# A hybrid decoder layer on one core: column blocks of the output projection paired at its begin and its end, and the last product in 256-column matmuls

## The chip, the core and the metric

The kernel runs on one core of a Trainium2 chip. Its engines are TensorE (PE, with its weight loads shown apart as PEld), VectorE (DVE), ScalarE (ACT), GpSimd (POOL) and SyncE (SP), which issues most of the DMAs. The metric is the device time of one execution in microseconds. Before the change the median of three runs was 1169.38 us (1169.16 to 1171.19).

## The reference

One layer over 256 tokens of width 2048, float32. What matters is the chain of four large products and the two layer norms, here in short:

```python
u = x @ w_in                                     # 2048 -> 6160, the first product
conv_out = conformer_conv_group(u[..., :1024], u[..., 1024:2048], ...)
gdn_out = gated_deltanet_group(u[..., c0:c1], u[..., c1:c2], ...)   # 8 heads, chunks of 64 tokens
mix = concat([conv_out, gdn_out]) @ w_out        # 2048 -> 2048, the second product
x = layer_norm(alpha * x + mix, ln1_g, ln1_b)
gu = x @ w_gate_up                               # 2048 -> 11264, the third product
hid = silu(gu[..., :D_FF]) * gu[..., D_FF:]      # D_FF = 5632
ffn = hid @ w_down                               # 5632 -> 2048, the fourth product
x = layer_norm(alpha * x + ffn, ln2_g, ln2_b)
```

Depth is 1, alpha is 2 to the power 0.25.

## The kernel before

Every large product is made of three matmuls on split operands: each float32 operand is cut into a high part (rounded to the type that TensorE takes) and a low part (what is left), and high by high, high by low and low by high are summed in PSUM.

**Weights.** A weight chunk is 256 rows by 512 columns, 512 KB. `wchunk` (L85 to L104) loads it by a DMA from SP into `wraw` (three buffers), ACT makes the high part `whi` (L93), DVE the low part `wlo` (L100); `whi` and `wlo` have four buffers each. A `wraw` buffer is free again when DVE has made the low part, a `whi` buffer when PE has used it. A program-wide scheduler orders the instructions of each engine by priority; weights are placed some 500 places ahead of their use (WPRI). Small pieces of the token mixer are queued with due times and run between chunks (`at`, `tick`, `require`).

**Second product.** Tokens (two halves `tk` of 128) are the stationary operand, 512 weight columns move. Its sum over 2048 rows is done in two passes: pass 0 takes the DeltaNet half (`mixg`), pass 1 the convolution half (`mixc`). `gemm2` (L723) runs one column block `nb` with four chunks `c`, both token halves in two PSUM banks `g2a`, `g2b`. Chunks 2 and 3 of pass 0 need the heads 4 to 7: `require(("gc"[pas], c // 2))`, which runs `head_mix` with its transposes `poT` (L615).

The last two column blocks of pass 1 are done differently (L802 to L829): all eight chunks stay in SBUF, those of block 2 in the four `whi`/`wlo` buffers, those of block 3 in four buffers of their own, `wxhi`/`wxlo`. Then token half 0 is run through blocks 2 and 3 (PSUM tiles `g2t`), its layer norm is started (`x1_stats`, `x1_norm`), and token half 1 is run through the same chunks, while the normed half 0 is transposed (`x1_turn`, tile `px1T`) to be the moving operand of the third product. The first chunks of the third product (`fxraw`, `fxhi`, `fxlo`, then `whi`) are loaded after those of the second.

**Third product.** Weights are stationary, 256 tokens move: 128x256 matmuls (L901), 22 column groups.

**Fourth product.** Tokens stationary again, 512 weight columns move (`tok_mm`), four column blocks of 22 chunks each, banks `g4a` and `g4b`, `evac4` adds the residual and takes the statistics. In the last block six chunks are held in SBUF: token half 0 is finished first and normed and stored (`finish`) while half 1 is multiplied, then half 1 is finished.

Of the kernel before, what the change touches and what calls it, by code (L numbers as in the profile page):

```python
# [14 lines left out]
P = 128  # L15
# [45 lines left out]
def hybrid_layer(ctx: ExitStack, tc, xT, xn, w1, wba, w2, w3, w4, pvec, consts, hrow, lrow, out):  # L61
# [18 lines left out]
    def mmt(name="mmt"):  # L80
        return mm.tile([P, 512], F32, tag="mm", name=name)
# [21 lines left out]
    def wchunk(src, split=False, into=None):  # L103
        return wrest(wload(src, split, into))  # L104
# [80 lines left out]
    def tick():  # L185
        while todo and todo[0][0] <= clock[0]:
            run_next()
        clock[0] += 1
# [3 lines left out]
    def require(key):  # L192
        while key not in done:
            run_next()
# [521 lines left out]

    def act_g(kt):
        return mixb[0][:, 0, kt, :], mixb[0][:, 1, kt, :]
# [4 lines left out]
    def gemm2(pas, nb):  # L723
        banks = [mmt("g2a"), mmt("g2b")]
        for c in range(4):
            hi, lo = wchunk(w2[pas, nb, c])
            require(("gc"[pas], c // 2))
            for k2 in range(2):
                for tk in range(2):
                    tok_mm(banks[tk], act_c if pas else act_g, 2 * c + k2, tk, hi, lo, k2, 8)  # L730
            tick()
        return banks
# [10 lines left out]
    for nb in range(4):  # L743
        banks = gemm2(0, nb)
        for tk in range(2):
            ysl = y[:, tk, nb * 512:nb * 512 + 512]
            STT(ysl, ysl, ALPHA, banks[tk], op0=ALU.mult, op1=ALU.add)
# [16 lines left out]
    for nb in range(2):  # L764
        banks = gemm2(1, nb)
        for tk in range(2):
            evac2(nb, tk, banks[tk])
# [3 lines left out]
    def x1_stats(tk):  # L771
        with tc.high_priority(offset=LPRI):
            m, r, nmr = ln_scalars(st1[:, tk], f"a{tk}")
            STT(nmr, m, -1.0, r, op0=ALU.mult, op1=ALU.mult)
        return m, r, nmr
# [26 lines left out]
    ws = {}  # L802
    for nb in (2, 3):
        for c in range(4):
            into = [pc.tile([P, 2, 512], F32R, tag=t, name=t, bufs=4) for t in ("wxhi", "wxlo")] if nb == 3 else None
            ws[nb, c] = wchunk(w2[1, nb, c], into=into)
    first = []
    for tk in range(2):
        for nb in (2, 3):
            if tk and nb == 3:  # L810
                for c in range(NF):
                    into = None
                    if c < NX:
                        into = [pc.tile([P, 2, 512], dt, tag=t, name=t, bufs=NX)
                                for t, dt in (("fxhi", F32R), ("fxlo", F32R), ("fxraw", F32))]
                    with tc.issue_after(loads[0].ins):
                        first.append(wload(w3[0, c], into=into))
            bank = mmt("g2t")
            for kt in range(8):
                tok_mm(bank, act_c, kt, tk, *ws[nb, kt // 2], kt % 2, 8)  # L820
                if tk and (nb, kt) in X1T:
                    with tc.issue_after(last[0].ins):
                        x1_turn(0, 4 * X1T.index((nb, kt)), 4)
            evac2(nb, tk, bank)
        sc1 = x1_stats(tk)
        hold = x1_norm(tk, 0, *sc1)
        if tk == 0:
            for b in range(1, 4):
                x1_norm(tk, b, *sc1)  # L829
# [89 lines left out]
    st2 = cp.tile([P, 2, 4, 6], F32, name="st2")  # L919
# [7 lines left out]
    def evac4(nb, tk, bank):  # L927
        sl = y[:, tk, nb * 512:nb * 512 + 512]
        STT(sl, sl, ALPHA, bank, op0=ALU.mult, op1=ALU.add)
        nc.vector.bn_stats(st2[:, tk, nb, :], sl)  # L930

    def finish(tk):
        m, r, _ = ln_scalars(st2[:, tk], f"b{tk}")
        for nb in range(4):
            sl = y[:, tk, nb * 512:nb * 512 + 512]
            STT(sl, sl, m, l2[:, 0, nb, :], op0=ALU.subtract, op1=ALU.mult)
            STT(sl, sl, r, l2[:, 1, nb, :], op0=ALU.mult, op1=ALU.add)
            nc.sync.dma_start(out[tk * P:tk * P + P, nb * 512:nb * 512 + 512], sl)

    NC4 = FT // 2  # L940
    wx = big.tile([P, 2, 2, 2, 512], F32R, tag="big", name="wx")
    for nb in range(4):
        banks = [mmt("g4a"), mmt("g4b")]
        held = 6 if nb == 3 else 0
        for c in range(NC4 - held):
            hi, lo = wchunk(w4[nb, c])
            for k2 in range(2):
                for tk in range(2):
                    tok_mm(banks[tk], act_h, 2 * c + k2, tk, hi, lo, k2, FT)
        ws = []  # L950
        for c in range(NC4 - held, NC4):
            i = c - (NC4 - held)
            ws.append(wchunk(w4[nb, c], into=(wx[:, i, 0], wx[:, i, 1]) if i < 2 else None))
        for tk in range(2):
            for kt in range(FT - 2 * held, FT):
                tok_mm(banks[tk], act_h, kt, tk, *ws[kt // 2 - NC4 + held], kt % 2, FT)
            evac4(nb, tk, banks[tk])
            if held:
                finish(tk)
# [10 lines left out]
NH0 = 1  # L970
X1T = [(2, 7), (3, 2), (3, 4), (3, 7)]
# [79 lines left out]
```

## Time and profile before

| | |
|---|---|
| median of 3 runs | 1169.38 us |
| profiled execution | 1173.28 us, its span 1171.5 us |
| PE busy | 1153.6 us (98%), 8514 matmuls |
| DVE, ACT, POOL busy | 63%, 48%, 3% |
| first product | 5.3 to 332 us |
| second product | 334 to 436 us |
| third product | 437 to 918 us |
| fourth product | 918 to 1160 us, then norm and store to 1171.5 us |

The profiled execution was 3.9 us slower than the median of the runs. PE is busy nearly all the time; a matmul's duration in the trace reaches past the start of the next one (they are pipelined), so a pace is read from start to start and not from a duration. Idle time in brackets names what ended it.

### The profile page before, as it was taken

The numbers are of one execution on the slowest core, as the hardware profiler recorded it, in microseconds if no ns is written. First come the engines' busy times: TensorE is split into PE (matmuls) and PEld (weight loads), VectorE is DVE, ScalarE is ACT, GpSimd is POOL, SyncE is SP. The second block draws the span as 40 slices with busy tenths as digits, with TensorE's granted clock in tenths as the row PEclk, the third lists the DMA queues.
The fourth block names the chain that finished last, engine by engine and source line by source line (L and its number), as shares of the span: only waits on it lengthen the run. The fifth ranks groups of instructions, "written<-read, shape, count | busy, mean of one in ns | idle before, by whom it ended". The sixth has DMA issues, their size and how long they took to land.

```text
span 1171.5 us, 20710 instructions
## 1 busy us (share of the span) xinstructions
PE 1153.6 (98%) x8514; PEld 1087.4 (93%) x8514; DVE 735.6 (63%) x1092; ACT 561.3 (48%) x803; POOL 34.9 (3%) x44
## 2 busy tenths in 40 slices
PE   9999999999999999999999999999999999999996
PEld 9999999999988879999999999999999888888884
DVE  5998998978847777545545455455554445454545
ACT  6567455556664544444444444444444333333340
POOL 1001011100000000000000000000000000000000
PEclk9999999999999999999999999999999999999998
DMA  8556564453535744655555555555555755555552
GB/s 292 182 190 214 176 210 156 153 196 127 198 129 177 263 150 159 217 191 192 197 195 191 194 195 197 191 191 196 197 194 192 264 187 190 197 189 189 197 202 86
DMA packets 62014, 222.65 MB, mean 190 GB/s; under 512 B 7168, under 2 KB 7680, under 8 KB 61280
## 3 DMA queue, kind: packets, MB, share of 16 engines
q1 hardware_dynamic: 58464, 208.37, 52.4%
q0 software_dynamic: 2160, 10.88, 2.8%
q10 hardware_dynamic: 1296, 2.10, 0.5%
q8 instruction: 66, 1.08, 0.4%
q14 instruction: 28, 0.23, 0.1%
HBM read 216.86 MB, written 4.46 MB: 189 GB/s over the span
## 4 chain that ended last, share of the span: by engine, by line
PE 71%; ACT 1%; DVE 1%; issue 1%; DMA 1%; POOL 0%; DVEq 0%; ACTq 0%
PE g3b L901 20%; PE g3a L901 20%; PE g4b L715 3%; PE g4a L715 3%; PE g4a L714 3%; PE g4b L714 3%; PE g4b L713 3%; PE g4a L713 3%; PE g1a L206 1%; PE g1b L206 1%; PE g2a L715 1%; PE g2a L713 1%; PE g2b L713 1%; PE g2a L714 1%; PE g2b L715 1%; PE g2b L714 1%
## 5 line engine op out<-in xcount | busy, mean ns | idle before, releaser
L100 DVE TENSOR_TENSOR wlo<-wraw,whi 128x1024 fp32r<-128x1024 f32 (+1 forms) x386 | 469.8, 1218 | 392.3 <-ACT whi L93 390.3
L93 ACT ACTIVATE whi<-wraw 128x1024 fp32r<-128x1024 f32 (+1 forms) x386 | 406.9, 1056 | 498.5 <-PE g3b L901 232.1
L901 PE MATMUL g3b<-x,whi 128*128 128x256 f32 x1344 | 261.7, 276 | 0.0
L901 PE MATMUL g3a<-x,whi 128*128 128x256 f32 x1344 | 261.6, 276 | 0.0
L901 PEld LDWEIGHTS g3a<-x,whi 128*128 128x128 f32 x1344 | 202.3, 188 | 0.0
L901 PEld LDWEIGHTS g3b<-x,whi 128*128 128x128 f32 x1344 | 202.3, 188 | 0.0
L901 PE MATMUL g3a<-x,wlo 128*128 128x256 f32 x672 | 130.8, 276 | 0.0
L901 PE MATMUL g3b<-x,wlo 128*128 128x256 f32 x672 | 130.8, 276 | 0.0
L639 DVE SCALAR_TENSOR_TENSOR cacc<-hh,pv,cacc 128x255 f32<-128x255 f32 (+27 forms) x240 | 100.8, 463 | 0.7 <-ACT cacc L636 0.7
L901 PEld LDWEIGHTS g3a<-x,wlo 128*128 128x128 f32 x672 | 101.2, 188 | 0.0
L901 PEld LDWEIGHTS g3b<-x,wlo 128*128 128x128 f32 x672 | 101.1, 188 | 0.0
L206 PE MATMUL g1a<-x_hi,whi 128*128 128x256 f32 x384 | 79.8, 290 | 0.9 <-ACT whi L93 0.5
L206 PE MATMUL g1b<-x_hi,whi 128*128 128x256 f32 x384 | 76.6, 281 | 0.0
L206 PE MATMUL g1a<-x_lo,whi 128*128 128x256 f32 x384 | 76.5, 281 | 0.0
L206 PE MATMUL g1b<-x_lo,whi 128*128 128x256 f32 x384 | 76.5, 281 | 0.0
L206 PE MATMUL g1a<-x_hi,wlo 128*128 128x256 f32 x384 | 76.4, 281 | 0.0
L206 PE MATMUL g1b<-x_hi,wlo 128*128 128x256 f32 x384 | 76.3, 280 | 0.0
L715 PE MATMUL g4b<-whi,hid 128*128 128x512 f32 x172 | 67.8, 394 | 0.0
L715 PE MATMUL g4a<-whi,hid 128*128 128x512 f32 x172 | 67.8, 394 | 0.0
L714 PE MATMUL g4a<-wlo,hid 128*128 128x512 f32 x172 | 67.4, 392 | 0.0
L714 PE MATMUL g4b<-wlo,hid 128*128 128x512 f32 x172 | 67.4, 392 | 0.0
L713 PE MATMUL g4a<-whi,hid 128*128 128x512 f32 x172 | 66.8, 388 | 0.0
(319 smaller groups left out, 1519.2 us busy)
## 6 DMA issues: line engine op xcount, KB each, us to landing
wraw<-in_w SPq DMA_DIRECT2D x388, 512.0 KB, 3.3
y<-in_xn POOLq DMA_DIRECT2D x1, 2048.0 KB, 8.5
rows<-in_lrow POOLq DMA_DIRECT2D x2, 1024.0 KB, 6.9
l<-in_lrow POOLq DMA_DIRECT2D x2, 1024.0 KB, 7.7
out<-y SPq DMA_DIRECT2D x8, 256.0 KB, 2.6
xr<-in_xT ACTq DMA_DIRECT2D x7, 256.0 KB, 5.4
wraw<-in_w SPq DMA_DIRECT2D x4, 256.0 KB, 4.1
dzx<-zbg POOLq DMA_DIRECT2D x2, 512.0 KB, 4.9
```

Of the source, the lines that this page charges most:

```text
L93: ACT(hi[:, k], raw[:, k], AF.Copy)
L100: TT(lo[:, k], raw[:, k], hi[:, k].bitcast(F32), op=ALU.subtract)
L206: last[0] = MM(o, lhsT=w[:, k2, ct * P:ct * P + P], rhs=r[:, kt, :], start=(kt == 0 and ct % 2 == 0 and r is r_hi and not fin), stop=(fin ...
L639: STT(a[:, s:], hh[:, i, :S - s], pcol(w + TAPS - 1 - s), a[:, s:], op0=ALU.mult, op1=ALU.add)
L713: MM(bank, lhsT=a_hi[:, tsl], rhs=hi[:, k2, :], start=(kt == 0), stop=False)
L714: MM(bank, lhsT=a_hi[:, tsl], rhs=lo[:, k2, :], start=False, stop=False)
L715: last[0] = MM(bank, lhsT=a_lo[:, tsl], rhs=hi[:, k2, :], start=False, stop=(kt == n - 1))
L901: last[0] = MM(banks[ct // 2][:, (ct % 2) * S:(ct % 2) * S + S], lhsT=w[:, k2, ct * P:ct * P + P], rhs=x1[kt // 8][:, kt % 8, part, :], st ...
```

## The change

Three edits. First, `gemm2` takes a tuple of column blocks and runs chunks 0 and 1 of all of them before chunks 2 and 3; the first two blocks of pass 0 are given as a pair. Second, at the end of pass 1 the eight chunks of blocks 2 and 3 are loaded and used, for token half 0, in an order of a table that mixes both blocks; token half 1 keeps its order. Third, the fourth product uses `half_mm`, in which each 512-column matmul is two of 256 columns, and in the held part of the last block token half 1 is finished in column halves; statistics of token half 1 are taken over 256 columns, and its last column block is normed and stored in two pieces.

```diff
+    def half_mm(banks, act, kts, tks, hfs, hi, lo, n):
+        for part, w in ((0, hi), (1, hi), (0, lo)):
+            for kt in kts:
+                for hf in hfs:
+                    cs = slice(hf * 256, hf * 256 + 256)
+                    for tk in tks:
+                        last[0] = MM(banks[tk][:, cs], lhsT=act(kt)[part][:, tk * P:tk * P + P], rhs=w[:, kt % 2, cs],
+                                     start=(kt == 0 and hf == 0 and part == 0 and w is hi),
+                                     stop=(w is lo and kt == n - 1), skip_group_check=True)
...
-    def gemm2(pas, nb):
-        banks = [mmt("g2a"), mmt("g2b")]
-        for c in range(4):
...
+    def gemm2(pas, nbs):
+        banks = {}
+        for half in range(2):
+            for nb in nbs:
+                if half == 0:
+                    banks[nb] = [mmt("g2a"), mmt("g2b")]
+                for c in (2 * half, 2 * half + 1):
+                    hi, lo = wchunk(w2[pas, nb, c])
+                    require(("gc"[pas], half))
...
-    for nb in range(4):
-        banks = gemm2(0, nb)
+    for nbs in ((0, 1), (2,), (3,)):
+        banks = gemm2(0, nbs)
...
+LASTW = [(2, 0), (3, 0), (2, 1), (2, 2), (3, 1), (2, 3), (3, 2), (3, 3)]
...
+    for nb, c in LASTW:
+        into = [pc.tile([P, 2, 512], F32R, tag=t, name=t, bufs=4) for t in ("wxhi", "wxlo")] if nb == 3 else None
+        ws[nb, c] = wchunk(w2[1, nb, c], into=into)
+    first = []
+    last_banks = {nb: mmt("g2t") for nb in (2, 3)}
+    for nb, c in LASTW:
+        for k2 in range(2):
+            tok_mm(last_banks[nb], act_c, 2 * c + k2, 0, *ws[nb, c], k2, 8)
+        if c == 3:
+            evac2(nb, 0, last_banks[nb])
...
-    st2 = cp.tile([P, 2, 4, 6], F32, name="st2")
+    st2 = [cp.tile([P, 4, 6], F32, name="st2a"), cp.tile([P, 8, 6], F32, name="st2b")]
...
-            for k2 in range(2):
-                for tk in range(2):
-                    tok_mm(banks[tk], act_h, 2 * c + k2, tk, hi, lo, k2, FT)
+            half_mm(banks, act_h, (2 * c, 2 * c + 1), (0, 1), (0, 1), hi, lo, FT)
...
+        for tk, hfs in ((0, (0, 1)), (1, (0,)), (1, (1,))):
+            for c in range(NC4 - held, NC4):
+                half_mm(banks, act_h, (2 * c, 2 * c + 1), (tk,), hfs, *ws[c - NC4 + held], FT)
+            evac4(nb, tk, banks[tk], hfs if tk else None)
+            if tk == 0:
+                finish(0, (0, 512, 1024, 1536, 2048))
+    finish(1, (0, 512, 1024, 1536, 1792, 2048))
```

The order of instructions shows where each part lands. First PE at the begin of the second product, pass 0, from the last matmul of block 0's chunk 1 to the first transpose `poT`. Before; `g2a_4380` and `g2b_4381` are block 0, `g2a_4514` and `g2b_4515` block 1:

```order
L715 MATMUL g2b_4381<-whi_4459,mixg_4088 128x512
L713 MATMUL g2a_4514<-whi_4517,mixg_4088 128x512
L714 MATMUL g2a_4514<-wlo_4518,mixg_4088 128x512
L715 MATMUL g2a_4514<-whi_4517,mixg_4088 128x512
L713 MATMUL g2b_4515<-whi_4517,mixg_4088 128x512
L714 MATMUL g2b_4515<-wlo_4518,mixg_4088 128x512
L715 MATMUL g2b_4515<-whi_4517,mixg_4088 128x512
L713 MATMUL g2a_4514<-whi_4517,mixg_4088 128x512
L615 MATMUL poT_4432<-con_81,vs_3702 128x128
```

And the same place with the change, where block 1 is `g2a_4476` and `g2b_4477`:

```order
L715 MATMUL g2b_4381<-whi_4459,mixg_4088 128x512
L713 MATMUL g2a_4476<-whi_4479,mixg_4088 128x512
L714 MATMUL g2a_4476<-wlo_4480,mixg_4088 128x512
L715 MATMUL g2a_4476<-whi_4479,mixg_4088 128x512
L713 MATMUL g2b_4477<-whi_4479,mixg_4088 128x512
L714 MATMUL g2b_4477<-wlo_4480,mixg_4088 128x512
L715 MATMUL g2b_4477<-whi_4479,mixg_4088 128x512
L713 MATMUL g2a_4476<-whi_4479,mixg_4088 128x512
L615 MATMUL poT_4432<-con_81,vs_3702 128x128
```

Nothing moved up to `poT`: the scheduler had put block 1's first chunk there before, too. What moves stands behind it.

Second, ACT at the end of the second product: the high parts of the eight chunks of blocks 2 and 3 (`whi` is block 2, `wxhi` block 3), between the last chunk of block 1 (`whi_4949`) and the first of the third product (`fxhi`). Before:

```order
L93 ACTIVATE whi_4949<-wraw_4948 128x1024
L93 ACTIVATE whi_4973<-wraw_4972 128x1024
L93 ACTIVATE whi_4979<-wraw_4978 128x1024
L93 ACTIVATE whi_4985<-wraw_4984 128x1024
L93 ACTIVATE whi_4991<-wraw_4990 128x1024
L93 ACTIVATE wxhi_4996<-wraw_4998 128x1024
L93 ACTIVATE wxhi_5002<-wraw_5004 128x1024
L93 ACTIVATE wxhi_5008<-wraw_5010 128x1024
L93 ACTIVATE wxhi_5014<-wraw_5016 128x1024
L93 ACTIVATE fxhi_5127<-fxraw_5129 128x1024
```

With the change:

```order
L93 ACTIVATE whi_4949<-wraw_4948 128x1024
L93 ACTIVATE whi_4973<-wraw_4972 128x1024
L93 ACTIVATE wxhi_4978<-wraw_4980 128x1024
L93 ACTIVATE whi_4985<-wraw_4984 128x1024
L93 ACTIVATE whi_4991<-wraw_4990 128x1024
L93 ACTIVATE wxhi_4996<-wraw_4998 128x1024
L93 ACTIVATE whi_5003<-wraw_5002 128x1024
L93 ACTIVATE wxhi_5008<-wraw_5010 128x1024
L93 ACTIVATE wxhi_5014<-wraw_5016 128x1024
L93 ACTIVATE fxhi_5127<-fxraw_5129 128x1024
```

The first load of block 3 stands second instead of fifth, and the last of block 2 sixth instead of fourth; SP's queue has the same order.

Third, DVE behind that, from the low part of the eighth chunk to the begin of the norm of token half 0 (L753, now L768, adds a PSUM bank to `y`). Before:

```order
L100 TENSOR_TENSOR wxlo_5015<-wraw_5016,wxhi_5014 128x1024
L100 TENSOR_TENSOR fxlo_5128<-fxraw_5129,fxhi_5127 128x1024
L753 TENSOR_TENSOR y_4378<-y_4378,g2t_5047 128x512
L100 TENSOR_TENSOR fxlo_5133<-fxraw_5134,fxhi_5132 128x1024
L754 BN_STATS st1_4806<-y_4378 128x6
L100 TENSOR_TENSOR wlo_5139<-wraw_5137,whi_5138 128x1024
L736 BN_AGGR mva0_5074<-st1_4806 128x2
```

With the change:

```order
L100 TENSOR_TENSOR wxlo_5015<-wraw_5016,wxhi_5014 128x1024
L100 TENSOR_TENSOR fxlo_5128<-fxraw_5129,fxhi_5127 128x1024
L768 TENSOR_TENSOR y_4378<-y_4378,g2t_5020 128x512
L100 TENSOR_TENSOR fxlo_5133<-fxraw_5134,fxhi_5132 128x1024
L769 BN_STATS st1_4806<-y_4378 128x6
L768 TENSOR_TENSOR y_4378<-y_4378,g2t_5021 128x512
L769 BN_STATS st1_4806<-y_4378 128x6
L750 BN_AGGR mva0_5074<-st1_4806 128x2
```

Block 2's addition and statistics, which stood further ahead, now stand behind the low part of the eighth chunk, and `wlo_5139` has gone behind the norm's first steps.

## Rows read from the trace of the kernel before

**Rows 1.** The page: busy time and share; DVE's busy tenths in 40 slices.

```profile
PE 1153.6 (98%) x8514; PEld 1087.4 (93%) x8514; DVE 735.6 (63%) x1092; ACT 561.3 (48%) x803; POOL 34.9 (3%) x44
...
DVE  5998998978847777545545455455554445454545
```

**Rows 2.** Waits of PE: who, for whom, us in total, times, longest.

```profile
PE g2t L713 <- ACT wxhi L93: 1.5, 1, 1.5
PE poT L615 <- ACT vs L586: 1.2, 1, 1.2
...
PE px1T L796 <- DVE y L785: 0.2, 1, 0.2
```

**Rows 3.** Timeline of PE, end of the second product: start us, us, instruction.

```profile
415.93 0.39 PE L715 MATMUL g2t<-wxhi,mixc 128*128 128x512 f32 x1
417.85 0.50 PE L713 MATMUL g2t<-wxhi,mixc 128*128 128x512 f32 x1 [1.53 <-ACT wxhi L93]
419.11 0.66 PE L714 MATMUL g2t<-wxlo,mixc 128*128 128x512 f32 x1 [0.76 <-DVE wxlo L100]
...
422.86 0.39 PE L713 MATMUL g2t<-wxhi,mixc 128*128 128x512 f32 x1
```

**Rows 4.** Windows there: PE, PEld, DVE, ACT, POOL busy, granted clock, DMA, GB/s.

```profile
420.00:425.00 5.00, 5.00 (x18) 3.99 (x17) 2.77 (x4) 1.44 (x3) 0.00 (x0) 0.73 0.64 216
```

**Rows 5.** Timeline of ACT there: the third, fourth and seventh of the eight chunks.

```profile
405.33 1.06 ACT L93 ACTIVATE whi<-wraw 128x1024 fp32r<-128x1024 f32 x1 [1.69 <-PE g2b L715]
408.08 1.06 ACT L93 ACTIVATE whi<-wraw 128x1024 fp32r<-128x1024 f32 x1 [1.69 <-PE g2b L715]
...
416.74 1.06 ACT L93 ACTIVATE wxhi<-wraw 128x1024 fp32r<-128x1024 f32 x1 [3.73 <-DMA wraw<-in_w]
```

**Rows 6.** Chain of waits there: the seventh chunk's DMA, issue and time.

```profile
410.60 6.12 DMA wraw<-in_w
```

**Rows 7.** SP there: the issue of the eighth chunk's DMA.

```profile
411.87 0.33 SPq L92 DMA_DIRECT2D wraw<-in_w  x1
```

**Rows 8.** DMAs into `wraw`, 395 to 425 us: issue to landing.

```profile
DMA to landing us min/median/max: 3.1/4.4/7.4
```

**Rows 9.** Timeline of DVE behind it: the norm of token half 0.

```profile
423.75 0.69 DVE L753 TENSOR_TENSOR y<-y,g2t 128x512 f32<-128x512 f32 x1 [2.21 <-PE g2t L715]
...
427.22 0.26 DVE L736 BATCH_NORM_AGGREGATE mva<-st 128x2 f32<-128x24 f32 x1
...
429.99 0.48 DVE L785 SCALAR_TENSOR_TENSOR y<-y,ra,rows 128x256 f32<-128x256 f32 x1
```

**Rows 10.** Windows, the matmuls of L901 alone: PE, PEld busy, clock, DMA, GB/s.

```profile
461.20:918.30 457.10, 457.01 (x4032) 457.01 (x4032) 1.00 0.59 200
```

**Rows 11.** Timeline of PE: first matmul of the fourth product, first of its held part.

```profile
918.25 0.39 PE L713 MATMUL g4a<-whi,hid 128*128 128x512 f32 x1
...
1143.47 0.39 PE L713 MATMUL g4a<-wx,hid 128*128 128x512 f32 x1
```

**Rows 12.** Timeline of PE: eight 512-column matmuls, then eight of 256.

```profile
455.74 0.39 PE L838 MATMUL g3a<-x,whi 128*128 128x512 f32 x1
...
457.60 0.28 PE L847 MATMUL g3a<-x,wlo 128*128 128x256 f32 x1
...
458.51 0.39 PE L838 MATMUL g3a<-x,whi 128*128 128x512 f32 x1
```

**Rows 13.** Timeline of PE, first product: sixteen 256-column matmuls from first to last row.

```profile
59.85 0.40 PE L206 MATMUL g1b<-x_hi,whi 128*128 128x256 f32 x2
...
61.74 0.40 PE L206 MATMUL g1b<-x_hi,wlo 128*128 128x256 f32 x2
```

**Rows 14.** Timeline of DVE after the last matmul.

```profile
1160.21 0.69 DVE L929 SCALAR_TENSOR_TENSOR y<-y,g4b 128x512 f32<-128x512 f32 x1 [1.09 <-PE g4b L715]
...
1163.36 1.41 DVE L937 SCALAR_TENSOR_TENSOR y<-y,rb,l 128x512 f32<-128x512 f32 x2
...
1166.01 1.41 DVE L937 SCALAR_TENSOR_TENSOR y<-y,rb,l 128x512 f32<-128x512 f32 x2
```

More of the change, by code (lines that the diff above doesn't have):

```diff
@@ L721, in act_c @@
         return mixc[kt][:, 0, :], mixc[kt][:, 1, :]
-    def gemm2(pas, nb):
-        banks = [mmt("g2a"), mmt("g2b")]
-        for c in range(4):
-            hi, lo = wchunk(w2[pas, nb, c])
-            require(("gc"[pas], c // 2))
-            for k2 in range(2):
-                for tk in range(2):
-                    tok_mm(banks[tk], act_c if pas else act_g, 2 * c + k2, tk, hi, lo, k2, 8)
-            tick()
+    def gemm2(pas, nbs):
[8 more added lines that the diff above has]
+                    for k2 in range(2):
+                        for tk in range(2):
+                            tok_mm(banks[nb][tk], act_c if pas else act_g, 2 * c + k2, tk, hi, lo, k2, 8)
+                    tick()
         return banks
@@ L742, in hybrid_layer @@
     at(clock[0] + CLN, conv_ln)
-    for nb in range(4):
-        banks = gemm2(0, nb)
-        for tk in range(2):
-            ysl = y[:, tk, nb * 512:nb * 512 + 512]
-            STT(ysl, ysl, ALPHA, banks[tk], op0=ALU.mult, op1=ALU.add)
+    for nbs in ((0, 1), (2,), (3,)):
+        banks = gemm2(0, nbs)
+        for nb in nbs:
+            for tk in range(2):
+                ysl = y[:, tk, nb * 512:nb * 512 + 512]
+                STT(ysl, ysl, ALPHA, banks[nb][tk], op0=ALU.mult, op1=ALU.add)
     st1 = cp.tile([P, 2, 4, 6], F32, name="st1")
@@ L764, in hybrid_layer @@
     for nb in range(2):
-        banks = gemm2(1, nb)
+        banks = gemm2(1, (nb,))[nb]
         for tk in range(2):
@@ L802, in hybrid_layer @@
     ws = {}
-    for nb in (2, 3):
[L804 to L829, printed above, removed]
@@ new lines, in hybrid_layer @@
+    for nb, c in LASTW:
[4 more added lines that the diff above has]
+    for nb, c in LASTW:
+        for k2 in range(2):
+            tok_mm(last_banks[nb], act_c, 2 * c + k2, 0, *ws[nb, c], k2, 8)
+        if c == 3:
+            evac2(nb, 0, last_banks[nb])
+    sc1 = x1_stats(0)
+    for b in range(4):
+        x1_norm(0, b, *sc1)
@@ new lines, in hybrid_layer @@
+    for nb in (2, 3):
+        if nb == 3:
+            for c in range(NF):
+                into = None
+                if c < NX:
+                    into = [pc.tile([P, 2, 512], dt, tag=t, name=t, bufs=NX)
+                            for t, dt in (("fxhi", F32R), ("fxlo", F32R), ("fxraw", F32))]
+                with tc.issue_after(loads[0].ins):
+                    first.append(wload(w3[0, c], into=into))
+        bank = mmt("g2t")
+        for kt in range(8):
+            tok_mm(bank, act_c, kt, 1, *ws[nb, kt // 2], kt % 2, 8)
+            if (nb, kt) in X1T:
+                with tc.issue_after(last[0].ins):
+                    x1_turn(0, 4 * X1T.index((nb, kt)), 4)
+        evac2(nb, 1, bank)
@@ L831, in g3_banks @@
+    sc1 = x1_stats(1)
+    hold = x1_norm(1, 0, *sc1)
     def g3_banks():
@@ L925, in act_h, with evac4, finish @@
         return hid[:, 0, kt, :], hid[:, 1, kt, :]
[L927 to L938, printed above, removed]
-    NC4 = FT // 2
+    NC4 = FT // 2
+    HELD = 6
+    st2 = [cp.tile([P, 4, 6], F32, name="st2a"), cp.tile([P, 8, 6], F32, name="st2b")]
+    def evac4(nb, tk, bank, hfs=None):
+        for hf in hfs or (0, 1)[:tk + 1]:
+            n = 256 if tk else 512
+            sl = y[:, tk, nb * 512 + hf * n:nb * 512 + hf * n + n]
+            STT(sl, sl, ALPHA, bank[:, hf * n:hf * n + n], op0=ALU.mult, op1=ALU.add)
+            nc.vector.bn_stats(st2[tk][:, nb * (tk + 1) + hf, :], sl)
+    def finish(tk, edges):
+        m, r, _ = ln_scalars(st2[tk], f"b{tk}")
+        g2, b2 = (l2[:, i].rearrange("p a b -> p (a b)") for i in range(2))
+        for lo, up in zip(edges, edges[1:]):
+            sl = y[:, tk, lo:up]
+            STT(sl, sl, m, g2[:, lo:up], op0=ALU.subtract, op1=ALU.mult)
+            STT(sl, sl, r, b2[:, lo:up], op0=ALU.mult, op1=ALU.add)
+            nc.sync.dma_start(out[tk * P:tk * P + P, lo:up], sl)
     wx = big.tile([P, 2, 2, 2, 512], F32R, tag="big", name="wx")
@@ L943, in hybrid_layer @@
         banks = [mmt("g4a"), mmt("g4b")]
-        held = 6 if nb == 3 else 0
+        held = HELD if nb == 3 else 0
         for c in range(NC4 - held):
             hi, lo = wchunk(w4[nb, c])
-            for k2 in range(2):
-                for tk in range(2):
-                    tok_mm(banks[tk], act_h, 2 * c + k2, tk, hi, lo, k2, FT)
+            half_mm(banks, act_h, (2 * c, 2 * c + 1), (0, 1), (0, 1), hi, lo, FT)
+        if not held:
+            for tk in range(2):
+                evac4(nb, tk, banks[tk])
+            continue
         ws = []
```

6 lines of the change are left out of this document (removed).

## The prediction, made before the result was known

> **What bounds the kernel now.** I read the page's first part first: PE is busy 98% of the span [rows 1], so time can come only from three places: where PE stands still or runs slowly, the pace of its matmuls, and what follows the last of them. The waits of PE are the second view. Over the whole span they are few; those that this change can reach are the wait of `g2t` for `wxhi` at the end of the second product, the wait of the transposes `poT` at its begin (1.2 us), and a short one of the transposes `px1T` [rows 2]. The third view, the timeline of PE around the `wxhi` wait, shows that it costs more than its idle time: after 415.93 the next matmul starts at 417.85, the one behind it at 419.11, and the normal pace is back only at 422.86 [rows 3], because the granted clock fell: 0.73 in the mean from 420 to 425 [rows 4]. That is a stretch at the lower of the two levels (1.2 GHz) behind PE's idle time. The fourth view is the pace from start to start.
>
> **Begin of the second product, 0.0 us.** The pair gives PE work of block 1 to do while heads 4 to 7 are finished. But the order before the change shows that work there already: the scheduler had drawn seven matmuls of block 1 ahead of `poT`, and with the change the same seven stand there. What `poT` waits for (ACT, DVE and POOL on those heads) keeps its order, so the 1.2 us wait stays [rows 2]. I take 0; at best the wait goes (1.2 us), at worst the two chunks moved behind it cost 0.6, half of it.
>
> **End of the second product, 2.6 us gained.** What is lost now: at the fourth product's pace of 228.9 ns (below) a matmul was due at 416.16; the pace is back at 422.86; ten matmuls start in between, worth 2.29 us. So 6.70 - 2.29 = 4.4 us are lost [rows 3].
>
> Why: token half 0 uses a chunk in six matmuls, 1.37 us, faster than chunks arrive, so it lives on what is ready. The third and fourth loads each waited 1.69 us for PE to free a `whi` buffer [rows 5]. The seventh load is issued when the fourth one's low part is done (three `wraw` buffers): at 410.60, and it took 6.12 us [rows 6]; ACT had idled 3.73 us when it landed [rows 5]. With the change a load of block 3 stands second, so the third and fourth take buffers that are free by then and wait for their DMA instead. I estimate the fourth chunk 1.4 us earlier (it landed before 408.08, and DVE need not first add block 1's banks), so the seventh is issued at about 409.2. The eighth stays at about 411.5, against 411.87 [rows 7], since the fifth, which frees its buffer, is hardly earlier. With the median time to landing of 4.4 us [rows 8], 1.06 us on ACT [rows 5] and 1.2 on DVE (with the hand-overs it was 1.3 from ACT's end at 417.80 to PE's start at 419.11 [rows 3, 5]), their low parts are ready at 415.9 and 418.2; PE, which does not stop before, wants them at 416.4 and 417.7. That is a stall of 0.5 us. With 6.1 us each, the time of the seventh before [rows 6], it is 2.2 us. I take 1.0, nearer to the median, and no fall of the clock behind so little.
>
> What is late next: the norm of token half 0. In DVE's queue the low parts of chunk eight and of the third product's first two chunks, and block 2's addition and statistics, now stand ahead of block 3's addition. From the start of chunk eight's low part that is three operations of 1.2 us, four of 0.6 (0.69 long, the next begins before the end), and then what the norm took before from its aggregation to the end of its second piece, 427.22 to 430.47 less an addition of 0.6 in between [rows 9]: 8.6 us, and 0.4 less to its first piece. PE, from the same point, has 1.2 us to wait and 28 matmuls to do, 7.6 us. So `px1T` waits some 0.7 us, where it waited 0.2 [rows 2]. Behind it `wlo_5139`, moved there, delays the next two groups of transposes by some 0.3. Together 0.8 us are given back: 4.4 - 1.0 - 0.8 = 2.6. The bounds are 0 (stall of 2.2 us and the clock low again behind it) and 4.4.
>
> The moved `wlo` also frees its `wraw` buffer later, so the last of the third product's first six chunks is loaded later; PE comes to that one only after 24 matmuls of 512 columns and 40 of 256, some 10 us on, against 4.4 us of DMA and 1.06 of ACT: hidden.
>
> **Pace of the fourth product, 2.6 us gained.** Before: 984 matmuls of 512 columns from 918.25 to 1143.47 [rows 11], 228.9 ns each. The 72 of the held part end at 1160.21 [rows 11, 14]; in all 241.96 us. A 256-column matmul with its own weight load costs 457.01 us / 4032 = 113.3 ns in the third product [rows 10], two of them 226.7. There weights are stationary and tokens move, here the other way round; so the best row is one stretch with both widths on the same operands: eight of 512 take 1.86 us from 455.74, the eight of 256 behind them 0.91 [rows 12], so 232.5 against two times 113.8 ns. The smaller matmul is the cheaper one per column, by 2%. 2112 x 113.3 = 239.4 us, a gain of 2.6. The low part of a chunk is now needed after sixteen matmuls, not after one; that only relaxes the weights, whose supply has no wait here. The other bound is the first product, where sixteen of 256 columns took 1.89 us, 118.1 ns [rows 13], with DVE busy nearly throughout (slices 2 to 10 of 40); it is busy about half the time in the third and the fourth product alike [rows 1], so I take the third's.
>
> The Trainium skill speaks against this part: "TensorE: Matmul & The Clock Gate", section "Back-to-back issue gap", gives a matmul of N columns N/2.4 + 2.5 ns, thus 215.8 ns for 512 and two times 109.2 for 256. By it the halves would cost 1056 x 2.5 = 2.6 us more, not 2.6 less, and the sum below would be 0.3 us. The trace disagrees on both widths (228.9 and 113.3 ns) and on which is dearer per column.
>
> **Tail, 0.3 us gained.** After the last matmul DVE adds 512 columns and takes their statistics; now only 256 of each are left, the other half being done under the last 36 matmuls (4.1 us; `finish(0)` with its additions, 7.2 us as its twin for half 1 [rows 14], is over before, half 1 lasting 8.2). A 256-column operation takes 0.48 us [rows 9], one of 512 took 0.69 [rows 14], and with the hand-over I take 0.25 saved twice, 0.5. From 1163.36 on six operations of 512 columns follow at 0.66 us (1163.36 to 1166.01 is four) [rows 14]; now four of 512 and four of 256 at 0.41, 0.3 us more. The last store has half the bytes: 0 to 0.3 us, I take 0.1. In all 0.3, bounds -0.2 and 0.8.
>
> **Sum.** 0 + 2.6 + 2.6 + 0.3 = 5.5 us. The profiled execution took 1173.28 us, so 1167.8 of its kind; the median of the runs is 3.9 us lower, 1169.4, and I hold the difference there: 1163.9 us.
>
> **Rivals.**
> - The stall at the end stays, with the clock behind it (13%). For it: the eighth load is hardly issued earlier, and the seventh's 6.12 us was no issue's fault. Against it: a load earlier in the queue meets a free buffer. The gain there is then 0.2 us, the whole 3.1: 1166.3.
> - No gain from the width (10%): a column costs the same, and the 2% of rows 12 belong to their stretch. Gain 2.9: 1166.5.
> - Slower (7%): a fixed cost per matmul, so that the fourth product's 2112 go at the first product's 118.1 ns [rows 13]. They take 249.4 us, 7.5 more than before; with 2.9 gained elsewhere the kernel ends 4.6 later, 1174.0. It decides from a pace of 115.9 ns on. Against it stands the third product's even pace over 4032 of them [rows 10]. The page's rule above is a milder form of it.
> - The pair at the begin does what it is for (8%): the 1.2 us wait goes, 1162.7.
> - The two statistics tiles take 96 bytes per partition more, so all tiles placed behind them move by 96 bytes. No row tells what that does to matmuls (4%): by the paces seen, 113.3 and 118.1 ns, it could matter either way. I set it at nothing.
>
> **How the numbers follow.** My forecast has 58%. Its own range is 1161 to 1166: the end of the second product between 0.6 and 4.4 us, the rest as bounded. Taking in the first two rivals and part of the third gives 1160.5 to 1168.5 for 8 in 10. A change under 0.2%, 2.3 us, can't be told from none here. Faster by more (under 1167.0) is the forecast, the pair, most of the first rival and half of the second: 0.81; within it 0.11; slower 0.08.
>
> **What the profile after should show.** `poT` still waits 1.2 us for ACT. Among PE's waits `wxhi` and `wxlo` sum to under 1.5 us, the granted clock holds 1.00 through the second product's end, and `px1T` waits somewhat longer than 0.2. The matmuls of the fourth product start 113.3 ns apart. From the last matmul to the first rescaling on DVE pass 2.6 us, not 3.15. I am wrong if the clock falls again behind a chunk's wait, or if the 256-column pace there lies over 115 ns.

## The result: 30 us slower, where 5.5 us faster was forecast

| | before | after |
|---|---|---|
| median of the runs, us | 1170.29 (4 runs, 1169.16 to 1171.27) | 1200.79 (4 runs, 1199.99 to 1201.70) |
| ratio, 95% interval | | 1.0259 [1.0246, 1.0272] |
| profiled execution, us | 1173.28 | 1201.70 |
| its span, us | 1171.5 | 1199.8 |

So 30.3 us were lost (28.8 to 31.8), against a forecast of 1163.9 and a range that ended at 1168.5. The page after answers to [rows 1]: PE is as full as before, with more busy time.

```profile
PE 1177.7 (98%) x9570; PEld 1153.7 (96%) x9570; DVE 736.3 (61%) x1102; ACT 561.2 (47%) x803; POOL 34.9 (3%) x44
...
DVE  5998998969658686454454554554454444454545
```

The waits of PE answer to [rows 2]. `wxhi` is gone and `poT` is as it was, both as forecast; the two waits for `wxlo` sum to 1.5 us, where under 1.5 was forecast. Two waits of `px1T` stand where 0.2 us stood, and on top is one that nobody had forecast: 3.4 us for DVE in the last block.

```profile
PE g4b L723 <- DVE y L953: 3.4, 1, 3.4
PE px1T L811 <- DVE y L804: 1.5, 1, 1.5
PE px1T L811 <- DVE y L800: 1.5, 1, 1.5
PE g2t L714 <- DVE wxlo L100: 1.5, 2, 0.8
PE poT L615 <- ACT vs L586: 1.2, 1, 1.2
```

Waits sum to a few us; most of the loss is pace. The window over the third product's matmuls alone (L901 before, L920 now) answers to [rows 10]: the same 4032 instructions in the same order, in code that the change doesn't touch, take 470.50 us and not 457.01. That is 116.7 ns each against 113.3, at a granted clock of 1.00 in both.

```profile
463.70:934.20 470.50, 470.50 (x4032) 470.35 (x4032) 1.00 0.60 195
```

The timeline of PE answers to [rows 11]: the first matmul of the fourth product, the first of its held part, and the end of that part.

```profile
934.09 0.28 PE L723 MATMUL g4a<-whi,hid 128*128 128x256 f32 x1
...
1166.97 3.03 PE L723 MATMUL g4a<-wx,hid 128*128 128x256 f32 x24
...
1179.55 0.40 PE L723 MATMUL g4b<-wlo,hid 128*128 128x256 f32 x2
1183.31 2.51 PE L723 MATMUL g4b<-wx,hid 128*128 128x256 f32 x12 [3.36 <-DVE y L953]
1185.62 1.05 PE L723 MATMUL g4b<-whi,hid 128*128 128x256 f32 x4
```

Ahead of the held part 1968 matmuls take 232.9 us, 118.3 ns each, where 113.3 was forecast; the prediction had named a pace over 115 ns as a sign of being wrong. Twelve matmuls from 1183.31 on take 2.3 us; twelve took 1.4 a little earlier. The clock fell behind the wait: here are the windows of that stretch, with the granted clock third from the end.

```profile
1180.00:1184.00 4.00, 0.69 (x5) 0.69 (x6) 3.69 (x7) 0.00 (x0) 0.00 (x0) 0.98 0.58 214
1184.00:1188.00 4.00, 4.00 (x23) 4.00 (x23) 0.00 (x0) 0.00 (x0) 0.00 (x0) 0.60 0.14 52
```

DVE's timeline answers to [rows 14]. What PE waits for is an addition of 0.42 us, which stands behind the rescalings of token half 0; the last addition comes at 1189.38.

```profile
1181.52 1.41 DVE L962 SCALAR_TENSOR_TENSOR y<-y,rb,l 128x512 f32<-128x512 f32 x2
1182.84 0.42 DVE L953 SCALAR_TENSOR_TENSOR y<-y,g4b 128x256 f32<-128x256 f32 x1
...
1189.38 0.42 DVE L953 SCALAR_TENSOR_TENSOR y<-y,g4b 128x256 f32<-128x256 f32 x1 [5.66 <-PE g4b L723]
```

At the end of the second product (PE's timeline, answering to [rows 3]) two short waits stand in place of the long one, then the two of `px1T`. The granted clock stays at 1.00 from 415 to 440 us, as forecast. The third product begins at 438.86; before it began at 436.57.

```profile
418.62 0.50 PE L714 MATMUL g2t<-wxlo,mixc 128*128 128x512 f32 x1 [0.76 <-DVE wxlo L100]
421.01 0.50 PE L714 MATMUL g2t<-wxlo,mixc 128*128 128x512 f32 x1 [0.73 <-DVE wxlo L100]
429.54 0.90 PE L811 MATMUL px1T<-con,y 128*128 128x128 f32 x4 [1.50 <-DVE y L800]
435.94 1.09 PE L811 MATMUL px1T<-con,y 128*128 128x128 f32 x8 [1.54 <-DVE y L804]
...
438.86 0.36 PE L857 MATMUL g3a<-x,fxhi 128*128 128x256 f32 x1
```

Laid end to end, from the starts just named and those of before (436.57; [rows 11, 14]):

| stretch | before, us | after, us | difference |
|---|---|---|---|
| start to first matmul of the third product | 436.6 | 438.9 | +2.3 |
| third product | 481.7 | 495.2 | +13.5 |
| fourth product up to the held part | 225.2 | 232.9 | +7.7 |
| held part, to the last addition's start | 16.7 | 22.4 | +5.7 |
| from there to the end of the span | 11.3 | 10.4 | -0.9 |
| span | 1171.5 | 1199.8 | +28.3 |

Three quarters of it, 21.2 us, is slower matmuls. The theory that the experiments start from: the two statistics tiles take 288 bytes where one took 192, so every tile placed behind them, `x`, `hid`, `mixc`, `y` and `wx` among them, starts 96 bytes further on, while the weight buffers `whi` and `wlo`, placed ahead of them, stay; that alone changes PE's pace. The rival: the changed orders and widths do it.

### The profile page after: what moved, and what is told of

Its sections match the earlier page's. It is cut to its first block, busy times and chain, and to the rows that moved or that the text cites. A ratio compares the mean times of both kernels' runs of the same rounds, so it can differ in the third digit from the quotient of the medians.

```text
span 1199.8 us, 22834 instructions
## 1 busy us (share of the span) xinstructions
PE 1177.7 (98%) x9570; PEld 1153.7 (96%) x9570; DVE 736.3 (61%) x1102; ACT 561.2 (47%) x803; POOL 34.9 (3%) x44
## 5 line engine op out<-in xcount | busy, mean ns | idle before, releaser
L920 PE MATMUL g3a<-x,whi 128*128 128x256 f32 x1344 | 267.8, 280 | 0.0
L920 PE MATMUL g3b<-x,whi 128*128 128x256 f32 x1344 | 262.9, 278 | 0.0
L920 PEld LDWEIGHTS g3b<-x,whi 128*128 128x128 f32 x1344 | 206.3, 188 | 0.0
L920 PEld LDWEIGHTS g3a<-x,whi 128*128 128x128 f32 x1344 | 204.0, 188 | 0.0
L723 PE MATMUL g4b<-whi,hid 128*128 128x256 f32 x688 | 164.7, 282 | 0.0
L723 PE MATMUL g4a<-whi,hid 128*128 128x256 f32 x688 | 163.6, 281 | 0.0
L920 PE MATMUL g3a<-x,wlo 128*128 128x256 f32 x672 | 133.9, 280 | 0.0
L920 PE MATMUL g3b<-x,wlo 128*128 128x256 f32 x672 | 131.5, 278 | 0.0
L723 PEld LDWEIGHTS g4b<-whi,hid 128*128 128x128 f32 x688 | 128.3, 189 | 0.0
L723 PEld LDWEIGHTS g4a<-whi,hid 128*128 128x128 f32 x688 | 128.0, 189 | 0.0
L920 PEld LDWEIGHTS g3b<-x,wlo 128*128 128x128 f32 x672 | 103.2, 188 | 0.0
L920 PEld LDWEIGHTS g3a<-x,wlo 128*128 128x128 f32 x672 | 102.0, 188 | 0.0
L723 PE MATMUL g4b<-wlo,hid 128*128 128x256 f32 x344 | 84.8, 282 | 0.0
L723 PE MATMUL g4a<-wlo,hid 128*128 128x256 f32 x344 | 84.1, 281 | 0.0
## 6 DMA issues: line engine op xcount, KB each, us to landing
rows<-in_lrow POOLq DMA_DIRECT2D x2, 1024.0 KB, 10.4
```

The lines of the kernel that those rows point to most:

```text
L723: last[0] = MM(banks[tk][:, cs], lhsT=act(kt)[part][:, tk * P:tk * P + P], rhs=w[:, kt % 2, cs], start=(kt == 0 and hf == 0 and part == 0 ...
L920: last[0] = MM(banks[ct // 2][:, (ct % 2) * S:(ct % 2) * S + S], lhsT=w[:, k2, ct * P:ct * P + P], rhs=x1[kt // 8][:, kt % 8, part, :], st ...
```

## The experiments

Ratios are to the kernel before, timed beside it on the same chip; a difference in us is the ratio's, of 1171.

### The place of the tiles

**pad96**: the kernel before, with the statistics tile longer by 24 floats.

```
-    st2 = cp.tile([P, 2, 4, 6], F32, name="st2")
+    st2 = cp.tile([P, 72], F32, name="st2")[:, 0:48].rearrange("p (a b c) -> p a b c", a=2, b=4)
```

> The kernel before with one edit: the statistics tile st2 is 96 bytes per partition longer, so every tile placed behind it moves by 96 bytes; the same instructions in the same order. Theory A (the place of the operands sets the pace): the third product's 4032 matmuls go from 113.3 to the 116.6 ns seen after the change, 13.6 us more, and the 512-column matmuls of the fourth from 228.9 to about 232.5, as the second product's did, 3.8 us more: about 1187 us. Theory B (something else that the change does, the order of the second product or the 256-column matmuls, slows PE): no change, 1169 to 1171 us.

Measured: 1.0160 [1.0146, 1.0174], 18.7 us more, median 1189.82. The third product's window has the changed kernel's number:

```profile
459.20:929.70 470.50, 470.42 (x4032) 470.44 (x4032) 1.00 0.58 195
```

The 984 matmuls of 512 columns ahead of the held part take 229.61 us (929.68 to 1159.29), 233.3 ns each against 228.9. Theory A holds, though its 1187 us fell short by 3; not one instruction differs.

**all96**: the kernel before, with the pad ahead of the weight buffers too.

```
+    pd = ctx.enter_context(tc.tile_pool(name="pd", bufs=1))
+    nc.gpsimd.memset(pd.tile([P, 24], F32, name="pad"), 0.0)
     wp = ctx.enter_context(tc.tile_pool(name="wp", bufs=4))
```

> The kernel before with a pad of 96 bytes ahead of all its tiles, so that x, hid and all the rest stand where they stood in the kernel with st2 lengthened by 96 bytes (1189.8 us, third product 116.6 ns), but the weight buffers wraw, whi and wlo move by 96 bytes too. Theory A (the distance between the places of the two operands of a matmul sets the pace): it is as before, third product 113.3 ns, 1169 to 1172 us. Theory B (the place of x and hid by itself sets it): third product 116.6 ns, 1187 to 1192 us. Theory C (any operand off a multiple of 64): as slow or slower than 1190 us.

Measured: 1.0004 [0.9993, 1.0016], no change. `x` and `hid` stand exactly where they stand in pad96; only the weights have moved along.

```profile
461.00:918.10 457.10, 457.01 (x4032) 457.01 (x4032) 1.00 0.60 200
```

So it is no place by itself: what counts is how far the tiles behind st2 lie from the weight buffers. That it is the distance of the two operands of a matmul, and not of other tiles in these two groups, is the simplest reading; the held part below bears it out.

**pad64** and **pad32**: as pad96, with 16 and 8 floats.

> The kernel before with st2 64 bytes longer; all later tiles move by 64 bytes, from 64 to 0 modulo 128. Theory A1 (a start that is a multiple of 64 is enough): third product 113.3 ns, fourth 228.9 per 512 columns, 1170 to 1171 us. Theory A2 (finer: the distance or the multiple of 128 matters): the third or the fourth product changes its pace by 1 to 4%, 5 to 25 us, in either direction.

> The kernel before with st2 32 bytes longer: all later tiles move by 32 bytes, those of x from 64 to 96 modulo 128, while whi and wlo stay at multiples of 128. So far the third product ran at 113.3 ns with x at 64 modulo 128, 116.6 at 32 and 120.0 at 0. Theory A1 (what counts is how far the starts of the two operands lie apart modulo 128, in either direction): 116.6 ns, some 13.5 us more in the third product, about 1184 to 1190 us. Theory A2 (the pace goes on falling in the same direction): 110 ns, 13.5 us less, about 1157 us. Theory A3 (only a start that is a multiple of 64 is fast, and 64-byte moves are a case of their own): 116.6 as well.

Measured: 1.0270 [1.0257, 1.0283] and 1.0248 [1.0234, 1.0262], 31.6 and 29.0 us more. The third product, pad32 and then pad64:

```profile
463.00:940.30 477.30, 477.16 (x4032) 477.19 (x4032) 1.00 0.56 192
```

```profile
466.00:949.80 483.80, 483.79 (x4032) 483.80 (x4032) 1.00 0.55 189
```

That is 118.3 and 120.0 ns. No theory of pad32 gave 118.3, and the theory that a multiple of 64 is enough fell. For pad64 A2 came true in kind, in both directions: its fourth product (949.85 to 1172.91) takes 226.7 ns per 512 columns, 2.2 less than before. In size it fell short: the third product is 5.9% or 26.8 us slower, where A2 went up to 4% and 25 us. Of the rest most is the first product, whose last matmul starts 7.8 us later in pad64 and 3.3 in pad32 than before.

**after_al**: the changed kernel, its second statistics tile longer by 8 floats (the move is then 128 bytes).

> The changed kernel with one edit: its second statistics tile is 32 bytes longer, so that all later tiles stand 128 bytes, not 96, behind their old places. Theory A (a start that is not a multiple of 64 bytes costs time): the third product is back at 113.3 ns per matmul, 13.6 us less, and the fourth below 118.3 ns: 1179 to 1187 us. Theory B (any move, or something else): 1200 us still. Under both the 3.4 us wait of PE in the held part stays.

Measured: 1.0150 [1.0130, 1.0170], median 1188.26, 12.5 us less than the changed kernel and just above the 1179 to 1187 of Theory A. The third product is back at 113.3 ns, the fourth is not: 117.8 (919.76 to 1151.55).

```profile
462.70:919.80 457.10, 457.00 (x4032) 457.02 (x4032) 1.00 0.61 200
```

### The width of 256 columns, and the place again

**halves**: the kernel before with `half_mm` in the fourth product (the held part too, token half by token half), all tiles in their places.

```
-            for k2 in range(2):
-                for tk in range(2):
-                    tok_mm(banks[tk], act_h, 2 * c + k2, tk, hi, lo, k2, FT)
+            half_mm(banks, act_h, (2 * c, 2 * c + 1), (0, 1), (0, 1), hi, lo, FT)
...
```

> The kernel before with the fourth product's matmuls at 256 columns each, ordered high by high, high by low, low by high, and nothing else: all tiles in their old places, the last block not split for its additions. Forecast's step (256 columns are the cheaper width): 113.3 ns, 2.6 us gained, about 1167 us. Rival (the width costs by itself): at the 118.3 ns of the changed kernel 8 us more, about 1177. Between: 114.5 ns, no change.

Measured: 0.9998 [0.9988, 1.0008], no change. The pace is the forecast one, 222.94 us for 1968, 113.3 ns:

```profile
916.40:1139.40 223.00, 222.94 (x1968) 223.00 (x1969) 1.00 0.61 197
```

In the traces this is worth 2.2 us up to the held part and 1.65 up to the last addition (240.31 us from 916.46 to 1156.77, against 241.96), since the held part costs 0.5 more (its matmuls go at 117.7 and 120.0 ns, see below). The timing allows a gain of 1.4 us at most. The rival, that the narrow width is slow by itself, has fallen: 1968 such matmuls go at 113.3 ns.

**halves_pad128**, **halves_pad256**, **halves_pad64**: the same with st2 longer by 32, 64 and 16 floats.

> The kernel before with 256-column matmuls in the fourth product and nothing else, and st2 128 bytes longer, so that all later tiles stand 128 bytes behind their old places. Theory A (the place of hid): the fourth product at 117.7 ns, 9 us more than without the move, about 1179 us; the third product at 113.3. Theory B (the rest of the change's code): 113.3 ns, about 1170 us.

> The kernel before with 256-column matmuls in the fourth product and st2 256 bytes longer. With the tiles 128 bytes behind their old places the third product kept its 113.3 ns, but the fourth went at 117.8 and the first nowhere at 113.3. Theory A (the distance of the two operands counts modulo 256): all as without a move, fourth product 113.3 ns, first product in part at 113.3, 1169 to 1172 us. Theory B (any move of these tiles from their old places costs the fourth product its pace; or the distance counts modulo 512 or more): 117.8 ns, about 1180 us.

> The kernel before with 256-column matmuls in the fourth product and st2 64 bytes longer: weights and hid then start at the same place modulo 128. With 512 columns that ran at 226.7 ns, less than the 228.9 of the old places, while the third product, at the same distance, went at 120.0 in place of 113.3. Theory A (the fourth product's narrow matmuls behave as the third's): 120 ns, 13 us more than at 512 columns, about 1214 us. Theory B (with the roles of weights and tokens exchanged the same distance is the fast one): 113.3 ns or less, 1200 to 1202 us.

Measured: 1.0102 [1.0087, 1.0117], 0.9995 [0.9986, 1.0005] and 1.0390 [1.0372, 1.0407]. The fourth product's windows in this order give 117.7, 113.3 and 120.0 ns:

```profile
918.30:1150.10 231.80, 231.71 (x1968) 231.80 (x1969) 1.00 0.56 191
```

```profile
916.50:1139.50 223.00, 222.96 (x1968) 223.00 (x1969) 1.00 0.60 197
```

```profile
949.50:1185.80 236.30, 236.30 (x1970) 236.30 (x1970) 1.00 0.57 186
```

In each of the three Theory A holds. A move of 256 bytes costs nothing, one of 128 costs the fourth product its pace and the third nothing.

The held part tells the two operands from all else. `wx`, the weights of two of the six held chunks, lies behind st2 like `hid`, so their distance stays when the tiles move. Here are, from PE's timelines of halves, halves_pad128 and halves_pad64, the first matmul with `wx`, the first with `whi` behind it, and the first of token half 1.

```profile
1139.50 3.04 PE L723 MATMUL g4a<-wx,hid 128*128 128x256 f32 x24
1142.38 1.11 PE L723 MATMUL g4a<-whi,hid 128*128 128x256 f32 x8
...
1148.03 3.05 PE L723 MATMUL g4b<-wx,hid 128*128 128x256 f32 x24
```

```profile
1150.17 3.03 PE L723 MATMUL g4a<-wx,hid 128*128 128x256 f32 x24
1153.05 1.09 PE L723 MATMUL g4a<-whi,hid 128*128 128x256 f32 x8
...
1158.51 3.02 PE L723 MATMUL g4b<-wx,hid 128*128 128x256 f32 x24
```

```profile
1185.58 3.04 PE L723 MATMUL g4a<-wx,hid 128*128 128x256 f32 x24
1188.46 1.12 PE L723 MATMUL g4a<-whi,hid 128*128 128x256 f32 x8
...
1194.22 3.04 PE L723 MATMUL g4b<-wx,hid 128*128 128x256 f32 x24
```

The 24 with `wx` take 2.88 us, 120.0 ns each, in all three. The 48 with `whi` and `wlo`, whose distance to `hid` changes, take 5.65, 5.46 and 5.76 us: 117.7 ns unmoved, 113.8 at 128 bytes, 120.0 at 64. So unmoved the held part has the slower pace and the rest of the product the faster (113.3), and at 128 bytes it is the other way round (117.7 in the rest); the held part runs one token half at a time, the rest both in turn. At 512 columns, with twelve matmuls at a time, the picture is less clean: in pad32 and pad96 `wx` keeps 227.5 to 230.0 ns beside 233.3 for `whi` and `wlo`, but in pad64 it goes at 226.7, where before it took 229.2 and 230.8.

**after_zero**: the changed kernel whole, with no tile moved.

```
-    st2 = [cp.tile([P, 4, 6], F32, name="st2a"), cp.tile([P, 8, 6], F32, name="st2b")]
+    st2 = [cp.tile([P, 2, 4, 6], F32, tag="st1", name="st2a")[:, 0],
+           cp.tile([P, 2, 4, 6], F32, tag="st2", name="st2b")[:, :].rearrange("p a b c -> p (a b) c")]
```

> The changed kernel whole, but the new statistics tiles take the places of st1 and of the old st2, so that no other tile moves. The kernel with the tiles 128 bytes behind their old places still ran the fourth product at 117.7 ns a matmul, where 256 columns in the old places ran at 113.3. Theory A (any move of hid costs there, 64 to 192 modulo 256 too): 113.3 ns in the fourth product, 8.7 us less than that kernel's 1188.3, about 1179 us. Theory B (something in the changed code slows the fourth product, not the place): 117.7 ns still, 1187 to 1189 us. Under both the third product runs at 113.3 and the 3.5 us wait in the held part stays.

Measured: 1.0064 [1.0051, 1.0077], median 1177.34; fourth product 113.3 ns (918.64 to 1141.68). Theory A: the place accounts for 23 of the 30 us. The 3.4 us wait is still there.

### The held part

**held_banks**: after_zero with a PSUM bank of its own for each column half of token half 1 in the last block.

```
...
+        if held:
+            banks[1] = [ps("g4c"), ps("g4d")]
...
```

> The changed kernel with no tile moved, and in the last block a PSUM bank of its own for each column half of token half 1, so that the matmuls of the second half need not wait until DVE has read the first. Theory A (the wait is for the shared tile, and DVE comes to it only after the eight rescalings of token half 0): the 3.4 us wait and the slow matmuls behind it go, about 5.5 us less than the 1177.3 us with the shared bank: 1171 to 1173 us. Theory B (DVE's queue sets the end anyway, 7 us of rescaling and then two additions): at most 2 us less, 1175 to 1177.

Measured: 1.0012 [1.0000, 1.0024], median 1172.28. Against the shared bank (after_zero) that is 5.1 us less by the medians and 6 by the ratios; in the traces the held part, up to the last addition's start, takes 17.3 us (1143.27 to 1160.55) in place of 22.4. Theory A. PE goes straight on, and DVE has done the first half just before the second is ready (timelines of PE and DVE):

```profile
1156.08 1.61 PE L724 MATMUL g4d<-wx,hid 128*128 128x256 f32 x12
```

```profile
1159.12 0.42 DVE L955 SCALAR_TENSOR_TENSOR y<-y,g4c 128x256 f32<-128x256 f32 x1
...
1160.55 0.42 DVE L955 SCALAR_TENSOR_TENSOR y<-y,g4d 128x256 f32<-128x256 f32 x1 [0.55 <-PE g4d L724]
```

### Begin and end of the second product

**pair**: the kernel before with blocks 0 and 1 in turn, and nothing else (`gemm2` and the loop behind it, as in the change).

> The kernel before with the begin of its second product alone changed (blocks 0 and 1 in turn), tiles in their old places. Forecast's step: nothing gained, poT still waits 1.2 us for ACT, 1169 to 1171.5 us. Rival: the wait goes, 1.2 us less. Rival: the two chunks that are moved behind the wait are late, 0.6 to 2 us more.

Measured: 1.0002 [0.9993, 1.0012]; `poT` waits 1.2 us. As forecast.

**lastw**: the kernel before with the new end of the second product alone (the `LASTW` loops, as in the change).

> The kernel before with the end of its second product alone in the new order (LASTW), tiles in their old places. Forecast's step: 2.6 us gained, about 1167 us, with waits for chunks of 1 us and the transposes px1T some 0.7 us. Rival (the gain goes into the waits of px1T, 3.0 us in the changed kernel, against 0.2): 1169 to 1171 us.

Measured: 1.0014 [1.0005, 1.0023], 1.6 us more. The waits of PE:

```profile
PE px1T L796 <- DVE y L789: 1.5, 1, 1.5
...
PE g2t L714 <- DVE wxlo L100: 1.0, 2, 0.8
...
PE px1T L796 <- DVE y L785: 0.4, 1, 0.4
PE g2t L713 <- ACT wxhi L93: 0.3, 1, 0.3
```

What it is to be held against is not the profile of before alone. Eleven profiles have the old end; the long wait for `wxhi` is in two of them (before 1.5, pair 1.4), not in the other nine. (Some of the nine run the second product at another pace; halves, best and all96 do not.) The first matmul of the third product in lastw, in before (with that wait) and in halves (the same order as before, without it), each behind a first product whose last matmuls started at 331.9 to 332.2:

```profile
436.69 0.36 PE L842 MATMUL g3a<-x,fxhi 128*128 128x256 f32 x1
```

```profile
436.57 0.36 PE L838 MATMUL g3a<-x,fxhi 128*128 128x256 f32 x1
```

```profile
434.78 0.36 PE L848 MATMUL g3a<-x,fxhi 128*128 128x256 f32 x1
```

So before, with the wait, is 1.8 us behind halves. But the idle time was the smaller part of that. In pair PE waits nearly as long, and the granted clock stays at 1.00 behind it, where before it fell to 0.73 [rows 4]; no other of the eleven shows a fall there.

```profile
420.00:425.00 5.00, 5.00 (x23) 4.05 (x23) 4.32 (x5) 2.99 (x3) 0.00 (x0) 1.00 0.71 257
```

From the start of the first product's last pair of matmuls to the third product's first matmul pass 102.8 us in halves, 103.1 in pair, 104.7 in before and 104.6 in lastw. The new order comes out where the old one did in its one profile with the low clock; `px1T` costs 1.9 us in lastw (1.5 + 0.4), and 1.5 us or more in all five profiles that have the new order.

### What helps, together

**best**: the kernel before with halves, and the last block in column halves with banks of their own; the second product as before.

> The kernel before with only those parts of the change that did no harm by themselves: 256-column matmuls in the fourth product, the last block finished in column halves with a PSUM bank of its own for each, the statistics tiles in old places; begin and end of the second product as before. If the parts add up: the fourth product's 113.3 ns in place of 114.45 (2.2 us) and the forecast's 0.3 us of the tail, 1168 to 1170 us against 1171. If the held part's rescalings sit in DVE's way as in the run before: 1170 to 1172.

Measured: 0.9996 [0.9986, 1.0005], median 1171.71 against 1172.26. No version here beats the kernel before by a measurable amount.

## Why the prediction was wrong, step by step

The step that cost most is the fifth below: the moved tiles, set at nothing, took 23 of the 30 us. The next is in the tail, some 5 to 6 us; the end of the second product has 1.6.

- **Begin of the second product, 0.** Right, in sign, size and reason (pair; `poT` 1.2 us).
- **End of the second product, 2.6 gained.** Wrong: 1.6 lost (0.6 to 2.7). Two terms failed. "So 6.70 - 2.29 = 4.4 us are lost" is true of the one profile [rows 3], but in nine of eleven that wait doesn't occur, and at the begin of the third product it made 1.8 us with the low clock and 0.3 without (pair). The time of the seventh chunk's DMA differs from execution to execution: 6.12 us in before [rows 6], some 4.2 in halves (issued at 411.82, taken up by ACT at 416.00), and I took one such time for the rule. The sign was there: the profiled execution was 3.9 us slower than the median of the runs, and the forecast carried that difference over whole, with a gain read from what was slow in it. And "delays the next two groups of transposes by some 0.3" was 1.5: between the second and the third piece of the norm DVE has not only `wlo_5139` (1.22 us) to do but an addition of half 1 and its statistics. The rest of the step held in lastw: the stall is 1.3 us for 1.0 forecast, the first `px1T` wait 0.4 for 0.7.
- **Pace of the fourth product, 2.6 gained.** The price was right ahead of the held part, for the old places alone: 113.3 ns in halves and after_zero, 118.3 in the changed kernel. In the held part it doesn't hold even there (117.7 and 120.0 ns in halves). And 0.2 of the 2.6 was no pace: the 241.96 us run on to DVE's addition, the 239.4 count matmuls alone. Of the gain the timing of halves finds none, with at most 1.4 us allowed; the traces say 1.65. The slower rival had the right number (118.1 for 118.3) for a wrong reason, by luck: there is no fixed cost per matmul, else halves would show it.
- **Tail, 0.3 gained.** The tail proper gained 0.9. The step that failed is the one left out: "`finish(0)` ... is over before, half 1 lasting 8.2" looked only at when DVE is needed at the end, not at who waits for DVE in between. Both column halves lie in one PSUM tile, so the second half's first matmul waits until DVE has read the first half, and that addition stands behind `finish(0)`. With the slow matmuls behind it the held part costs 5.7 us more; held_banks gets 5 to 6 back.
- **The moved tiles, "I set it at nothing", 4%.** This was the case: 23 us by after_zero against the whole change. "No row tells" was not quite true. [Rows 13] show 118.1 ns and [rows 10] 113.3 for the same instruction on operands from the same two pools (`wp` and `big`), and I explained the difference by DVE's load. Twelve microseconds later in the same first product of before, with DVE busy throughout, sixteen matmuls take 1.81 us, 113.1 ns:

```profile
72.06 0.39 PE L206 MATMUL g1a<-x_lo,whi 128*128 128x256 f32 x2
...
73.87 0.39 PE L206 MATMUL g1a<-x_hi,whi 128*128 128x256 f32 x2
```

So DVE wasn't the reason, and a pace that no engine explains was a warning that something outside the rows sets it. An edit that moves every operand deserved the bound that these two paces give: the 6144 matmuls of the third and the fourth product by 4.8 ns, 29 us, and a range to match.

The sum, by the ratios: 23 for the place (to after_zero) and 6 for the held part (from there to held_banks) leave 1.4 of the 30.3 us. The parts that held_banks still has, each measured by itself, come to 1.6: 1.6 for the second product's end, 0.2 for its begin, -0.2 for the width. Each of these has 1 us or more of noise either way, and the tail's gain was not timed by itself.

## What to carry to other kernels

A tile that grows by some bytes moves all that lie behind it; where PE is the bound, compare the starts of both operands before and after, and keep their distance (here by letting the new tile take a dead one's place). When a tile is to be finished in parts, give each part a buffer of its own, or the producer waits for the reader of the first. Before a wait is priced from one profile, see in others of the same order whether it recurs.

## What the runs showed of the hardware

Pace of PE against the bytes by which the tiles of tokens (`x`, `hid`) stand behind their old places, the weights staying; ns per matmul, granted clock 1.00. In the third product the weights are stationary and the tokens move through the array, in the fourth it is the other way round.

| moved by, bytes | third, 256 columns | fourth ahead of the held part, 256 | the same, 512 |
|---|---|---|---|
| 0 | 113.3 | 113.3 | 228.9 |
| 32 | 118.3 | - | 233.3 |
| 64 | 120.0 | 120.0 | 226.7 |
| 96 | 116.7 | 118.3 | 233.3 |
| 128 | 113.3 | 117.7 | - |
| 256 | 113.3 | 113.3 | - |
| 96, weights too | 113.3 | - | 228.9 |

The distance counts, and 256 bytes more make no difference. That a distance can be good at 512 columns and the worst at 256 (64 bytes) I had not expected. The formula that the prediction took from the Trainium skill, "TensorE: Matmul & The Clock Gate", section "Back-to-back issue gap", comes to 109.2 ns for 256 columns. The section calls it the gap of an isolated matmul; in the streams here no placement held a pace below 113 ns, and the measured paces stand.

What stays open: why the distance matters, and why one place can have two paces. In the first product of before stretches at 113.3 and at 117.8 ns alternate, and change where other matmuls come in between; with the tiles moved by 128 bytes only the slower one is left there, while the third product keeps the faster. The held part has it the other way round from the rest of the fourth product (117.7 and 113.3 ns unmoved, 113.8 and 117.7 at 128 bytes). So the distance alone does not settle the pace, and the order of the matmuls seems to have a part in it; no run tried that. Open too is why halves and best, 1.65 and 2.4 us shorter in their traces (240.3 us of fourth product in both, 0.8 of tail in best), are not measurably shorter in time.
